# A fifth K pair with seven products in gate/up chunks 7 and 9, its sums of weights made during the output projection

## The chip, the cores and the metric

One core of a Trainium2 chip runs the whole program in one launch. The metric is the time on the device in microseconds. Beside the plain times there is one profiled execution; all views come from it.

## What is computed

A trunk of two layers over 256 tokens of width 2048, in float32. Each layer has a mixer (two kinds of attention) and a SwiGLU feed-forward part, each between two RMS norms:

```python
for l in range(DEPTH):                      # 2
    h = rms_norm(x, pre_mix_norm[l])
    m = hybrid_mixer(h, ...)                # h @ w_in, attention, @ w_o
    x = x + rms_norm(m, post_mix_norm[l])
    h = rms_norm(x, pre_ffn_norm[l])
    f = (silu(h @ w_gate[l]) * (h @ w_up[l])) @ w_down[l]
    x = x + rms_norm(f, post_ffn_norm[l])
```

The change is about `h @ w_gate` and `h @ w_up`: 256 x 2048 times 2048 x 5632, twice.

## The kernel before

**Products.** Weights come as tiles of 256 rows of K (a *pair* of 128-row blocks, `kp` 0 to 7 for K = 2048) by 512 columns, as [128, 2, 512] in SBUF. A float32 weight is split into a rounded part `hi` (ScalarE, a copy with rounding) and a rest `lo` (VectorE, weight minus `hi`); the activations are split likewise. One product of a 128-row block with 128 tokens is then three matmuls in `product` (lines 1051 to 1053): high by `hi`, high by `lo`, low by `hi`, each with 512 columns.

**Eight or seven products.** In the gate/up stage a *chunk* is 512 columns of gate and the same of up; there are 11 a layer. For each chunk and pair there are 2 blocks of K, 2 halves of the tokens and 2 weights: eight products, 24 matmuls (`eight`). For some pairs the kernel uses a scheme of the Strassen-Winograd kind with seven products, 21 matmuls (`seven`, `seven_products`). In place of gate and up it then multiplies the gate blocks and four sums of weights: T1 (gate's first block plus up's first), B22 (up's second block), T2 = B22 − T1, and T3, T4 = gate's blocks + T2; and on the token side four sums made once per pair (`pair_sums`, `token_sums`). `gate_sevens(c)` says which pairs: 4, 6 in chunk 0; 4, 5, 6 in chunk 1; 2, 4, 5, 6 in the others.

**How the sums of weights are made.** For a pair with seven products the gate tile goes to a buffer `G` (three of them) and the up tile to a buffer `T` (four), both by DMAs on SyncE's queue; a DMA of GpSimd with addition then adds gate's first block onto T's first (`summed`, lines 237 and 238). `mixed_weights` (lines 243 to 274) does the rest: `hi`, `lo` of G and of T; T2 in place in T (128x512, line 267); G plus T2 in place in G (128x1024, line 268); then `Th`, `Tl` of T2 (128x512) and of G (128x1024), lines 259 and 260. For a pair with eight products the two tiles go to `raw` buffers (four) and get `hi` and `lo` (lines 286 and 289), two 128x1024 operations each on ScalarE and VectorE. `hi` and `lo` have six buffers, `Th` and `Tl` two.

**Order.** All weights have one order of use, `weight_order`. `weights(i, ahead)` feeds the splits of tile i and of four tiles more. `fetch` issues their loads and looks four tiles further for sums (`EARLY`). Each engine works through its own instructions in a written order, which the framework's scheduler chose by priorities (program order) and its own estimates. Some edges are given by hand: `not_ahead` (a load for sums goes behind the load of the usual tile six places before it), `after_rests` (a VectorE operation goes behind the newest `lo`), `in_turn` (a load goes behind the newest load). A clock of *ticks*, advanced in the program every few matmuls, starts side jobs written as generators (`start`, `tick`).

**Around the stage.** The output projection comes first: 8 pairs of K for four chunks of 512 columns; two chunks in a first half (16 units of 12 matmuls, two ticks each), two in a second, in which two pairs have seven products. At its end the residual x is normed, transposed and split into the columns `xF` that the gate/up stage multiplies by (lines 455 and 460). A pool at the right end of SBUF holds 16 column tiles, first those of the input projection, then `xF`. Four "late rooms" of 4 KB a partition hold the halves of x until they are put away in DRAM in chunks 3 to 6, then the `act` tiles of the chunks from 7 on.

Of the kernel before, what the change touches and what calls it, by code (L numbers as in the profile page):

```python
# [9 lines left out]
F32 = mybir.dt.float32  # L10
# [7 lines left out]
P = 128  # L18
D = 2048
S = 256  # L20
# [23 lines left out]
FIRST_SEVEN = (4, 6)  # L44
FIRST_ORDER = (0, 1, 3, 2, 7, 4, 6, 5)
NEXT_SEVEN = (4, 5, 6)
FORM_AT = {(0, 1): 4, (0, 2): 6, (0, 5): 5, (1, 3): 2}
DOWN_SEVEN = ((4, 7, 10, 12, 15, 17, 20), (3, 5, 8, 10, 13, 15, 18))

WARM = 10  # L50
# [8 lines left out]
    return 0.8 - 0.6 * math.exp(-0.3 * layer)  # L59


def gate_sevens(c):

    return (FIRST_SEVEN, NEXT_SEVEN)[c] if c < 2 else SEVEN


# [87 lines left out]
def kernel(  # L154
# [42 lines left out]
    def fetch(upto):  # L197
        while len(raws) < min(upto, len(stream)):
            i = len(raws)
            for j in range(i, min(i + EARLY + 1, mix_raw[3])):  # L200
                if j in sevens and j not in sums:
                    summed(j)
            if i in sevens:
                raws.append(sums[i])
                continue
            if i + 1 in sevens:
                g = mix_raw[0].tile([P, 2, CW], F32, tag="G", bufs=mix_raw[1], name=f"G{i}")
                with not_ahead(i):
                    loads.append(nc.sync.dma_start(g, stream[i]))
# [12 lines left out]
            if not mixing:  # L222
                usual.append((i, loads[-1]))
# [5 lines left out]
        return tc.issue_after(next(load.ins for j, load in reversed(usual) if j <= i - LEAD))  # L229

    sums = {}

    def summed(i):

        sums[i] = mix_raw[0].tile([P, 2, CW], F32, tag="T", bufs=mix_raw[2], name=f"T{i}")
        with not_ahead(i):
            loads.append(nc.sync.dma_start(sums[i], stream[i]))
        nc.gpsimd.dma_start(sums[i][:, 0, :], stream[i - 1][:, 0, :], accum_op=ALU.add)  # L238
# [4 lines left out]
    def mixed_weights(i):  # L243

        g, u = raws[i - 1], raws[i]
        hi = wpool.tile([P, 2, CW], F32R, tag="hi", bufs=6, name=f"hi{i}")
        lo = wpool.tile([P, 2, CW], F32R, tag="lo", bufs=6, name=f"lo{i}")
        if i in own:
            th = wpool.tile([P, 2, CW], F32R, tag="hi", bufs=6, name=f"Th{i}")
            tl = wpool.tile([P, 2, CW], F32R, tag="lo", bufs=6, name=f"Tl{i}")  # L250
            th2 = mix_pool[0].tile([P, 2 * (S + P)], F32R, tag="ah", bufs=1, name=f"T2h{i}")[:, 0:CW]
            tl2 = mix_pool[0].tile([P, 2 * (S + P)], F32R, tag="al", bufs=1, name=f"T2l{i}")[:, 0:CW]
        else:
            th = mix_pool[0].tile([P, 3, CW], F32R, tag="Th", bufs=1 if i in plain else 2, name=f"Th{i}")
            tl = mix_pool[0].tile([P, 3, CW], F32R, tag="Tl", bufs=1 if i in plain else 2, name=f"Tl{i}")
            th2, tl2 = th[:, 2, :], tl[:, 2, :]

        def split(h, l, w):
            nc.scalar.activation(h, w, AF.Copy)  # L259
            nc.vector.tensor_tensor(out=l, in0=w, in1=h.bitcast(F32), op=ALU.subtract)  # L260

        if i in plain or i in own:
            with after_rests():
                nc.vector.tensor_tensor(out=u[:, 0, :], in0=g[:, 0, :], in1=u[:, 0, :], op=ALU.add)
        split(hi, lo, u)
        t2 = u[:, 1, :]
        nc.vector.tensor_tensor(out=t2, in0=t2, in1=u[:, 0, :], op=ALU.subtract)  # L267
        nc.vector.tensor_tensor(out=g, in0=g, in1=t2.unsqueeze(1).to_broadcast([P, 2, CW]), op=ALU.add)  # L268
        split(th2, tl2, t2)
        split(th[:, 0:2, :], tl[:, 0:2, :], g)  # L270
        t1, b22 = ((hi[:, k, :], lo[:, k, :]) for k in range(2))
        t3, t4 = ((th[:, k, :], tl[:, k, :]) for k in range(2))
        t2 = th2, tl2
        return {"b22": b22, "t1": t1, "t2": t2, "t3": t3, "t4": t4}

# [779 lines left out]
    def token_sums(pool, spool, bufs, a11, a12, a21, a22, nm, tags=("sh", "sl")):  # L1055

        s = pool.tile([P, 4, P], F32, tag="t2", name=f"s{nm}")
        nc.vector.tensor_tensor(out=s[:, 0, :], in0=a21, in1=a22, op=ALU.add)
        nc.vector.tensor_tensor(out=s[:, 1, :], in0=s[:, 0, :], in1=a11, op=ALU.subtract)
        nc.vector.tensor_tensor(out=s[:, 2, :], in0=a11, in1=a21, op=ALU.subtract)  # L1060
        nc.vector.tensor_tensor(out=s[:, 3, :], in0=a12, in1=s[:, 1, :], op=ALU.subtract)
        sh = spool.tile([P, 4, P], F32R, tag=tags[0], bufs=bufs, name=f"sh{nm}")
        nc.scalar.activation(sh, s, AF.Copy)
        sl = spool.tile([P, 4, P], F32R, tag=tags[1], bufs=bufs, name=f"sl{nm}")
        nc.vector.tensor_tensor(out=sl, in0=s, in1=sh.bitcast(F32), op=ALU.subtract)
        return [(sh[:, j, :], sl[:, j, :]) for j in range(4)]

# [30 lines left out]
    for l in range(L):  # L1098
# [15 lines left out]
        for n, (c, kp) in enumerate(plan[l]["order_o"][:16]):  # L1114
# [5 lines left out]
            if n in (9, 11):  # L1120
                kp = O_SEVEN[(n - 9) // 2]
                forms[kp] = pair_forms(pool, pool, 4, mix, kp, f"o{l}", tags=("tok", "tok"))
        xT = x_tiles(f"xF{l}")
        got = four_banks(True, [f"o{l}_{c}_{t}" for t in range(NT) for c in (2, 3)])
        accs = {(c, t): got[2 * t + c - 2] for c in (2, 3) for t in range(NT)}
        open_sums[0] = True
        for kp in LATE_O:
# [49 lines left out]
        def pair_sums(kp):  # L1177
            f = pool.tile([P, 2, S], F32, tag="t2", name=f"f{l}_{kp}")
            for kk in range(2):
                st = xT[2 * kp + kk]  # L1180
                nc.vector.tensor_tensor(out=f[:, kk, :], in0=st[:, 0, :].bitcast(F32), in1=st[:, 1, :].bitcast(F32), op=ALU.add)
            forms[kp] = token_sums(pool, gu, len(SEVEN), f[:, 0, 0:P], f[:, 1, 0:P], f[:, 0, P:S], f[:, 1, P:S], f"{l}_{kp}")
# [228 lines left out]
```

## Time and profile before

| | us |
|---|---|
| median of 3 runs | 2191.08 (2190.44 to 2192.06) |
| the profiled execution | 2190.85 |
| its span, first to last instruction | 2189.1 |
| input projection and attention, layer 0 | 0 to about 297 |
| output projection, layer 0 | about 297 to 391 |
| gate/up stage, layer 0 | about 402 to 860 |
| chunk 7 of it, by VectorE's last step of a chunk | 691.1 to 732.9 |
| chunk 9 of it | 774.6 to 816.4 |

In the views PE is TensorE's matmuls, PEld its loads of stationary tiles, DVE VectorE, ACT ScalarE, POOL GpSimd, SPq the DMA queue of SyncE. A row of a timeline has the start in us from the span's start, the duration, engine, line, operation, what it writes and reads, shapes and count; a bracket at its end gives how long the engine was idle before it and what ended the wait. A row of a group has busy time in us, the mean of one in ns, and the idle time before. Matmuls are pipelined, so that the duration of one is longer than the distance to the next.

### The profile page before, as it was taken

The numbers are of one execution on the slowest core, as the hardware profiler recorded it, in microseconds if no ns is written. First come the engines' busy times: TensorE is split into PE (matmuls) and PEld (weight loads), VectorE is DVE, ScalarE is ACT, GpSimd is POOL, SyncE is SP. The second block draws the span as 40 slices with busy tenths as digits, with TensorE's granted clock in tenths as the row PEclk, the third lists the DMA queues.
The fourth block names the chain that finished last, engine by engine and source line by source line (L and its number), as shares of the span: only waits on it lengthen the run. The fifth ranks groups of instructions, "written<-read, shape, count | busy, mean of one in ns | idle before, by whom it ended". The sixth has DMA issues, their size and how long they took to land.

```text
span 2189.1 us, 28547 instructions
## 1 busy us (share of the span) xinstructions
PE 2175.5 (99%) x9992; PEld 1789.9 (82%) x9992; DVE 1900.6 (87%) x2609; ACT 1371.9 (63%) x2053; POOL 139.2 (6%) x187
## 2 busy tenths in 40 slices
PE   9999999999999999999999999999999999999998
PEld 7888888888888888888878888888888888888886
DVE  7888658999999999989878886589999999999997
ACT  7666665766656656666665656657665666566664
POOL 2100000010010010000010000000000000100000
PEclk9999999999999999999999999999999999999999
DMA  9545554587687676767465555555867867767683
GB/s 331 184 164 173 192 187 170 186 276 230 223 270 228 200 257 203 248 207 261 147 241 173 182 175 182 193 170 193 274 209 252 254 214 232 234 213 234 207 265 100
DMA packets 138545, 467.28 MB, mean 213 GB/s; under 512 B 15760, under 2 KB 16784, under 8 KB 137888
## 3 DMA queue, kind: packets, MB, share of 16 engines
q1 hardware_dynamic: 121952, 436.03, 57.0%
q0 software_dynamic: 15872, 28.88, 7.5%
q8 instruction: 78, 1.28, 0.2%
q14 instruction: 67, 0.55, 0.1%
q10 hardware_dynamic: 576, 0.54, 0.1%
HBM read 457.00 MB, written 8.39 MB: 213 GB/s over the span
## 4 chain that ended last, share of the span: by engine, by line
PE 94%; DVE 3%; ACT 1%; DMA 1%; issue 1%; DVEq 0%; ACTq 0%
PE c L1052 9%; PE c L1053 9%; PE c L1051 9%; PE in L1051 7%; PE in L1053 7%; PE in L1052 7%; PE dn L1292 4%; PE dn L1295 4%; PE dn L1293 4%; PE p L1052 2%; PE p L1053 2%; PE p L1051 2%; PE o L536 2%; PE o L537 2%; PE o L538 2%; DVE lo L289 1%
## 5 line engine op out<-in xcount | busy, mean ns | idle before, releaser
L289 DVE TENSOR_TENSOR lo<-raw,hi 128x1024 fp32r<-128x1024 f32 x522 | 625.0, 1218 | 97.1 <-ACT hi L286 95.9
L286 ACT ACTIVATE hi<-raw 128x1024 fp32r<-128x1024 f32 x522 | 540.6, 1055 | 187.0 <-issue 51.4
L1051 PE MATMUL c<-hi,xF 128*128 128x512 f32 x834 | 328.0, 394 | 0.1
L1052 PE MATMUL c<-lo,xF 128*128 128x512 f32 x834 | 325.1, 390 | 0.7 <-DVE lo L289 0.7
L1053 PE MATMUL c<-hi,xF 128*128 128x512 f32 x834 | 324.8, 390 | 0.0
L238 POOL DMA_DIRECT2D T<-in_weights_in_turn_dram x110 | 95.8, 871 | 1681.6 <-PE c L1052 521.5
L1052 PEld LDWEIGHTS c<-lo,xF 128*128 128x128 f32 x834 | 156.7, 188 | 33.5 <-DVE lo L289 2.5
L1053 PEld LDWEIGHTS c<-hi,xF 128*128 128x128 f32 x834 | 156.6, 188 | 32.7
L1051 PEld LDWEIGHTS c<-hi,xF 128*128 128x128 f32 x834 | 156.7, 188 | 31.5 <-ACT xF L455 0.5
L1292 PE MATMUL dn<-hi,jh 128*128 128x512 f32 x432 | 168.2, 389 | 0.0
L1293 PE MATMUL dn<-lo,jh 128*128 128x512 f32 x432 | 168.1, 389 | 0.0
L289 DVE TENSOR_TENSOR lo<-G,hi 128x1024 fp32r<-128x1024 f32 x110 | 134.0, 1218 | 29.8 <-ACT hi L286 29.8
L259 ACT ACTIVATE hi<-T 128x1024 fp32r<-128x1024 f32 x110 | 115.5, 1050 | 41.1 <-PE c L1053 26.5
L259 ACT ACTIVATE Th<-G 128x1024 fp32r<-128x1024 f32 x110 | 116.1, 1055 | 39.0 <-DVE G L268 37.1
L260 DVE TENSOR_TENSOR Tl<-G,Th 128x1024 fp32r<-128x1024 f32 x110 | 133.9, 1217 | 5.3 <-ACT Th L259 5.3
L260 DVE TENSOR_TENSOR lo<-T,hi 128x1024 fp32r<-128x1024 f32 x110 | 133.9, 1217 | 2.6 <-ACT hi L259 2.2
L268 DVE TENSOR_TENSOR G<-G,T 128x1024 f32<-128x1024 f32 x110 | 134.3, 1221 | 2.1
L259 ACT ACTIVATE Th<-T 128x512 fp32r<-128x512 f32 x110 | 68.9, 626 | 105.0 <-DVE T L267 89.1
L1295 PE MATMUL dn<-hi,jl 128*128 128x512 f32 x432 | 132.9, 390 | 0.0
L1051 PE MATMUL in<-hi,xT 128*128 128x512 f32 x328 | 131.0, 401 | 1.5 <-ACT hi L856 1.5
L1051 PE MATMUL in<-hi,xI 128*128 128x512 f32 x328 | 131.1, 401 | 0.0
L1052 PE MATMUL in<-lo,xI 128*128 128x512 f32 x328 | 128.0, 390 | 0.3 <-DVE lo L289 0.3
(456 smaller groups left out, 4734.5 us busy)
## 6 DMA issues: line engine op xcount, KB each, us to landing
raw<-in_weights_in_turn_dram SPq DMA_DIRECT2D x522, 512.0 KB, 4.5
T<-in_weights_in_turn_dram SPq DMA_DIRECT2D x110, 512.0 KB, 6.3
G<-in_weights_in_turn_dram SPq DMA_DIRECT2D x110, 512.0 KB, 5.8
T<-in_weights_in_turn_dram POOLq DMA_DIRECT2D x110, 256.0 KB, 7.1
GU<-in_weights_in_turn_dram SPq DMA_DIRECT2D x32, 512.0 KB, 6.4
V<-in_weights_in_turn_dram SPq DMA_DIRECT2D x8, 512.0 KB, 4.2
away_ffn<-x SPq DMA_DIRECT2D x8, 512.0 KB, 8.5
xd<-away_ffn SPq DMA_DIRECT2D x8, 512.0 KB, 8.6
```

The source lines that it names most:

```text
L238: nc.gpsimd.dma_start(sums[i][:, 0, :], stream[i - 1][:, 0, :], accum_op=ALU.add)
L259: nc.scalar.activation(h, w, AF.Copy)
L260: nc.vector.tensor_tensor(out=l, in0=w, in1=h.bitcast(F32), op=ALU.subtract)
L268: nc.vector.tensor_tensor(out=g, in0=g, in1=t2.unsqueeze(1).to_broadcast([P, 2, CW]), op=ALU.add)
L286: nc.scalar.activation(hi, raw, AF.Copy)
L289: rest = nc.vector.tensor_tensor(out=lo, in0=raw, in1=hi.bitcast(F32), op=ALU.subtract)
L1051: nc.tensor.matmul(a, sh, hi, start=first, stop=False, skip_group_check=open_sums[0])
L1052: nc.tensor.matmul(a, sh, lo, start=False, stop=False, skip_group_check=open_sums[0])
L1053: nc.tensor.matmul(a, sl, hi, start=False, stop=last, skip_group_check=open_sums[0])
L1292: nc.tensor.matmul(accs[c, t], sh, hi[:, kk, :], start=first, stop=False, skip_group_check=open_sums[0])
L1293: nc.tensor.matmul(accs[c, t], sh, lo[:, kk, :], start=False, stop=False, skip_group_check=open_sums[0])
L1295: nc.tensor.matmul(accs[c, t], sl, hi[:, kk, :], start=False, stop=last, skip_group_check=open_sums[0])
```

## The change

Pair 3 also gets seven products, in chunks 7 and 9 of both layers. Its sums T1, T2, T3 and T4 for these two chunks are not made there. During the output projection a generator, `foresee`, started 8 ticks after the mixer's program, loads gate and up tiles of both, makes the sums in place on VectorE and stores them in a DRAM tile by GpSimd's DMAs. The four tiles for this lie in the pool of the columns, which is opened anew for them and once more for `xF`. In chunks 7 and 9 `summed` loads for such a pair T1 (from DRAM), B22 (from the weights) into one T buffer, T2 into a late room, and T3 with T4 into a second T buffer; GpSimd adds nothing, and VectorE only splits. These loads are issued at most one tile ahead instead of four. Gate's tile goes to G as for the other sevens. The token sums of pair 3 are made in chunk 6, and are kept in a late room.

```diff
+MORE_SEVEN = (2, 3, 4, 5, 6)
+MORE_AT = (7, 9)
+FORESEEN = {7: (3,), 9: (3,)}
+AHEAD_AT = 8
+AHEAD_PACE = 4
-FORM_AT = {(0, 1): 4, (0, 2): 6, (0, 5): 5, (1, 3): 2}
+FORM_AT = {(0, 1): 4, (0, 2): 6, (0, 5): 5, (1, 3): 2, (6, 3): 3}
...
 def gate_sevens(c):
 
+    if c in MORE_AT:
+        return MORE_SEVEN
...
-                if j in sevens and j not in sums:
+                if j in sevens and j not in sums and not (j in foreseen and j > i + 1):
                     summed(j)
...
+    def foresee(l):
+
+        jobs = [plan[l]["up"][c, kp] for c, kp in FORESEEN_PER_LAYER]
+        tiles = {}
+
+        def summed_up(i):
+            g, u = tiles[i]
+            k = kept.tile([P, 4, CW], F32, name=f"foreseen{i}")
+            with after_rests():
+                sums_in_place(g, u, True)
+            nc.gpsimd.dma_start(k[:, 0:2, :], u)
+            nc.gpsimd.dma_start(k[:, 2:4, :], g)
+            foreseen[i] = k
+
+        for n, i in enumerate(jobs):
+            tiles[i] = [x_pool[0].tile([P, 2, CW], F32, tag="W", bufs=2 * len(jobs), name=f"{q}{i}") for q in ("Gf", "Tf")]
+            for t, j in zip(tiles[i], (i - 1, i)):
+                with in_turn():
+                    nc.sync.dma_start(t, stream[j])
+                yield AHEAD_PACE
+            if n:
+                summed_up(jobs[n - 1])
+            yield AHEAD_PACE
+        yield AHEAD_PACE
+        summed_up(jobs[-1])
+
+    def sums_in_place(g, u, first):
+
+        t2 = u[:, 1, :]
+        if first:
+            nc.vector.tensor_tensor(out=u[:, 0, :], in0=g[:, 0, :], in1=u[:, 0, :], op=ALU.add)
+        nc.vector.tensor_tensor(out=t2, in0=t2, in1=u[:, 0, :], op=ALU.subtract)
+        nc.vector.tensor_tensor(out=g, in0=g, in1=t2.unsqueeze(1).to_broadcast([P, 2, CW]), op=ALU.add)
...
     def summed(i):
 
+        if i in foreseen:
+            kept_sums = foreseen[i]
+            n = len(found)
+            if n % len(FORESEEN_PER_LAYER) == 0:
+                thirds.append(late_room([P, 2, CW], f"second{i}"))
+            second = thirds[-1][:, n % 2, :]
+            two = [mix_raw[0].tile([P, 2, CW], F32, tag="T", bufs=mix_raw[2], name=f"{q}{i}") for q in ("T", "W")]
+            with not_ahead(i):
+                loads.append(nc.sync.dma_start(two[0][:, 0, :], kept_sums[:, 0, :]))
+                loads.append(nc.sync.dma_start(two[0][:, 1, :], stream[i][:, 1, :]))
+                loads.append(nc.sync.dma_start(second, kept_sums[:, 1, :]))
+                loads.append(nc.sync.dma_start(two[1], kept_sums[:, 2:4, :]))
+            sums[i] = two[0]
+            found[i] = second, two[1]
+            return
...
         split(hi, lo, u)
+        t1, b22 = ((hi[:, k, :], lo[:, k, :]) for k in range(2))
+        t3, t4 = ((th[:, k, :], tl[:, k, :]) for k in range(2))
+        if i in found:
+            second, w = found[i]
+            split(th2, tl2, second)
+            split(th[:, 0:2, :], tl[:, 0:2, :], w)
+            return {"b22": b22, "t1": t1, "t2": (th2, tl2), "t3": t3, "t4": t4}
...
-        sh = spool.tile([P, 4, P], F32R, tag=tags[0], bufs=bufs, name=f"sh{nm}")
+        if spool is None:
+            both = late_room([P, 2, 4, P], f"ss{nm}", F32R)
+            sh, sl = both[:, 0], both[:, 1]
+        else:
+            sh = spool.tile([P, 4, P], F32R, tag=tags[0], bufs=bufs, name=f"sh{nm}")
+            sl = spool.tile([P, 4, P], F32R, tag=tags[1], bufs=bufs, name=f"sl{nm}")
...
         mixer_in(pool, l, rs, xT, mix, mixed)
+        new_x_pool(f"ahead{l}")
+        start(foresee(l), AHEAD_AT)
...
-        xT = x_tiles(f"xF{l}")
...
+        new_x_pool(f"xF{l}")
+        xT = x_tiles(f"xF{l}")
         idx = plan[l]["o"][2, LAST_O[0]]
...
-            forms[kp] = token_sums(pool, gu, len(SEVEN), f[:, 0, 0:P], ...)
+            forms[kp] = token_sums(pool, gu if kp in SEVEN else None, len(SEVEN), f[:, 0, 0:P], ...)
```

More of the change, by code (lines that the diff above doesn't have):

```diff
@@ L59, in lambda_init @@
     return 0.8 - 0.6 * math.exp(-0.3 * layer)
+FORESEEN_PER_LAYER = [(c, kp) for c in FORESEEN for kp in FORESEEN[c]]
 def gate_sevens(c):
+    if c in MORE_AT:
+        return MORE_SEVEN
     return (FIRST_SEVEN, NEXT_SEVEN)[c] if c < 2 else SEVEN
@@ L231 @@
     sums = {}
-    def summed(i):
+    foreseen, found, thirds = {}, {}, []
+    def foresee(l):
[26 more added lines that the diff above has]
+        nc.vector.tensor_tensor(out=g, in0=g, in1=t2.unsqueeze(1).to_broadcast([P, 2, CW]), op=ALU.add)
+    def summed(i):
+        if i in foreseen:
[13 more added lines that the diff above has]
+            return
         sums[i] = mix_raw[0].tile([P, 2, CW], F32, tag="T", bufs=mix_raw[2], name=f"T{i}")
@@ L270, in mixed_weights @@
         split(th[:, 0:2, :], tl[:, 0:2, :], g)
-        t1, b22 = ((hi[:, k, :], lo[:, k, :]) for k in range(2))
-        t3, t4 = ((th[:, k, :], tl[:, k, :]) for k in range(2))
         t2 = th2, tl2
@@ L1143 @@
                     nc.vector.tensor_tensor(out=accs[c, 1], in0=accs[c, 1], in1=mg[1, 1][:, c - 2, :], op=shared_sign(1, c - 2))
+        assert all(plan[l]["up"][at] in foreseen for at in FORESEEN_PER_LAYER)
+        new_x_pool(f"xF{l}")
+        xT = x_tiles(f"xF{l}")
         idx = plan[l]["o"][2, LAST_O[0]]
@@ L1181, in pair_sums @@
                 nc.vector.tensor_tensor(out=f[:, kk, :], in0=st[:, 0, :].bitcast(F32), in1=st[:, 1, :].bitcast(F32), op=ALU.add)
-            forms[kp] = token_sums(pool, gu, len(SEVEN), f[:, 0, 0:P], f[:, 1, 0:P], f[:, 0, P:S], f[:, 1, P:S], f"{l}_{kp}")
+            forms[kp] = token_sums(pool, gu if kp in SEVEN else None, len(SEVEN), f[:, 0, 0:P], f[:, 1, 0:P], f[:, 0, P:S], f[:, 1, P:S], f"{l}_{kp}")
         def eight(banks, c, kp, toks, first, last):
```

1 line of the change is left out of this document (removed).

## The prediction

> **What bounds the kernel now.** I read the page first, then the windows cut by gate/up chunk, then the timelines of TensorE and VectorE inside one chunk. Part 1 of the page:
>
> ```profile
> span 2189.1 us, 28547 instructions
> PE 2175.5 (99%) x9992; PEld 1789.9 (82%) x9992; DVE 1900.6 (87%) x2609; ACT 1371.9 (63%) x2053; POOL 139.2 (6%) x187
> PE 94%; DVE 3%; ACT 1%; DMA 1%; issue 1%; DVEq 0%; ACTq 0%
> ```
>
> PE is busy all the time, and the chain that ended last (third line) is PE for 94%. So a matmul taken out is worth its pitch, if nothing else then comes late. VectorE is the candidate: 87% over the span, and more where the change works. Chunks 7 and 9 of layer 0 in the windows (columns: window, length, PE, PEld, DVE, ACT, POOL, clock, DMA share, GB/s):
>
> ```profile
> 691.10:732.90 41.80, 41.80 (x190) 34.61 (x190) 39.05 (x43) 25.29 (x29) 2.99 (x5) 1.00 0.70 224
> 774.60:816.40 41.80, 41.80 (x190) 34.62 (x190) 39.05 (x43) 25.29 (x29) 3.75 (x5) 1.00 0.70 226
> ```
>
> A chunk takes 41.8 us on a PE without gaps at full clock; DVE works 39.05 of them and has 2.7 us left. ACT is far from its limit.
>
> **What a pair is worth on PE.** First matmuls of pairs 3 (eight products, 24 matmuls), 4 (seven products, 21 matmuls) and 5 of chunk 7:
>
> ```profile
> 709.53 0.39 PE L1051 MATMUL c<-hi,xF 128*128 128x512 f32 x1
> 714.97 0.39 PE L1051 MATMUL p<-hi,xF 128*128 128x512 f32 x1
> 719.73 0.39 PE L1051 MATMUL p<-hi,xF 128*128 128x512 f32 x1
> ```
>
> Pair 3 takes 5.44 us, pair 4 takes 4.76: 0.2267 us a matmul either way (the 0.39 of a row overlaps its neighbours). The change turns pair 3 into a seven in chunks 7 and 9 of both layers: four pairs, 12 matmuls, **−2.72 us**, and that is all the change can take from PE. The Trainium skill, page "TensorE: Matmul & The Clock Gate", section "Back-to-back issue gap", gives some 131 ns as the sustained spacing of matmuls with 512 columns; by that the 12 would be worth an estimated 1.57 us. Those rows disagree at 227 ns, and the measurement decides.
>
> **What it costs on VectorE in the two chunks.** Timeline of DVE in chunk 7 around pairs 3 to 6, as it is:
>
> ```profile
> 700.20 2.35 DVE L289 TENSOR_TENSOR lo<-raw,hi 128x1024 fp32r<-128x1024 f32 x2
> ...
> 705.41 1.23 DVE L289 TENSOR_TENSOR lo<-G,hi 128x1024 fp32r<-128x1024 f32 x1 [1.73 <-ACT hi L286]
> ...
> 710.69 1.22 DVE L260 TENSOR_TENSOR lo<-T,hi 128x1024 fp32r<-128x1024 f32 x1
> 711.82 0.68 DVE L260 TENSOR_TENSOR Tl<-T,Th 128x512 fp32r<-128x512 f32 x1
> 712.43 1.22 DVE L260 TENSOR_TENSOR Tl<-G,Th 128x1024 fp32r<-128x1024 f32 x1
> ...
> 725.17 1.22 DVE L260 TENSOR_TENSOR Tl<-G,Th 128x1024 fp32r<-128x1024 f32 x1
> ```
>
> From start to start a 128x1024 operation takes 1.135 us (two in 2.27) and a 128x512 one 0.61. An eight costs DVE two of the former, 2.27 us (the first row is pair 3). The added pair comes with its sums made, so it has no add, subtract or broadcast add here: lo of the gate tile, lo of T1 and B22, Tl of T2 (128x512), Tl of T3 and T4 = 3 × 1.135 + 0.61 = 4.01 us, so +1.74 us. PE gives it 0.68 us less time: against PE, VectorE loses 2.42 us of lead at pair 3. A chunk's total still fits (39.05 + 1.74 = 40.8 us in 41.1), but where the lead runs out counts: three sevens in a row (4, 5, 6) eat it already. The last Tl of pair 6 (725.17 + 1.22 = 726.39) is read by
>
> ```profile
> 726.76 0.39 PE L1052 MATMUL p<-Tl,sh 128*128 128x512 f32 x1
> ```
>
> 0.37 us later. After the change five sevens stand in a row. What covers the loss is the 1.73 us in which DVE waits at 705.41 (there it is ahead as far as its buffers let it): 2.42 − 1.73 − 0.37 = **0.32 us late at pair 6, four times: +1.27 us**. Ends: nothing, if PE or VectorE take their work in another order (the lo's of pairs 7 and 0, which DVE does between pair 6's operations, aren't urgent); 2.42 − 0.37 = 2.05 a chunk, 8.2 us, if the idle isn't used. The nearest row where such a run did come late is chunk 1, pair 5:
>
> ```profile
> 471.63 0.40 PE L1053 MATMUL c<-hi,sl 128*128 128x512 f32 x1
> 472.50 0.50 PE L1052 MATMUL p<-Tl,sh 128*128 128x512 f32 x1 [0.48 <-DVE Tl L260]
> ```
>
> 873 ns where 227 are usual: 0.65 lost. My 0.32 is nearer to that than to the far end, so I take it.
>
> ACT gets one more 128x512 Th in such a chunk,
>
> ```profile
> L259 ACT ACTIVATE Th<-T 128x512 fp32r<-128x512 f32 x110 | 68.9, 626 | 105.0 <-DVE T L267 89.1
> ```
>
> 0.63 us, in 16 us that it has to spare: nothing.
>
> **Token sums of pair 3, made in chunk 6.** Nearest rows: the same sums of another pair early in the stage.
>
> ```profile
> 417.60 0.75 DVE L1181 TENSOR_TENSOR f<-xF 128x256 f32<-128x256 f32 x2
> 418.27 0.29 DVE L1060 TENSOR_TENSOR s<-f 128x128 f32<-128x128 f32 x1
> 418.47 0.29 DVE L1058 TENSOR_TENSOR s<-f 128x128 f32<-128x128 f32 x1
> ...
> 422.29 0.69 DVE L1065 TENSOR_TENSOR sl<-s,sh 128x512 fp32r<-128x512 f32 x1
> 422.89 1.22 DVE L268 TENSOR_TENSOR G<-G,T 128x1024 f32<-128x1024 f32 x1
> ```
>
> 0.67 + 4 × 0.20 + 0.60 = 2.07 us of DVE, once a layer. They go behind pair 3's rests, thus into the same 1.73 us of idle time: 0.34 over, against pair 6's 0.37 of lead. I take nothing. Ends: nothing, and 2.07 − 0.37 = 1.70 a layer if the idle is missed. Their place and that of T2 are late-room tiles; the saved halves of x that held these leave one by one in chunks 3 to 6, and the act tiles of chunks 7 and 8 find two free: no wait.
>
> **Sums made ahead, in the output projection.** Per layer: four 512 KB loads on SP, six DVE operations (2 × (0.61 + 0.61 + 1.135) = 4.7 us), four 512 KB stores on POOL. Beside them stand
>
> ```profile
> 297.00:391.00 94.00, 94.00 (x452) 78.75 (x451) 68.28 (x105) 55.04 (x109) 0.00 (x0) 1.00 0.51 171
> 354.02 2.35 DVE L289 TENSOR_TENSOR lo<-raw,hi 128x1024 fp32r<-128x1024 f32 x2
> 361.09 0.39 PE L537 MATMUL o<-lo,mix_sb 128*128 128x512 f32 x1
> ```
>
> 25 us of idle DVE, a POOL that does nothing, half of the DMA engines' time, and weights that are ready before they are used: the first lo of the row at 354.02 ends at 355.24, 5.85 us ahead of its matmul, in one of the tightest places of the stage. One set of sums is 2.36 us, less than that lead: nothing on PE. On SP the loads go behind the newest weight load, 0.4 us of issue each; on POOL nothing stands behind the stores until the first accumulate at 410.4 (row of L238, below). The end of it: 36 ticks after the start, 1.36 us each (six matmuls), some 50 us after 297, so about 350. The columns' tiles that take the place of the loaded ones are written from
>
> ```profile
> 392.65 0.37 ACT L455 ACTIVATE xF<-xT_ps,gains 128x128 fp32r<-128x128 f32 x1 [1.03 <-PE xT_ps L452]
> ```
>
> on, so that a store has some 40 us to land. Ends: nothing, and 2.36 us a layer, for the one set that would meet an exhausted lead.
>
> **Loads in chunks 7 and 9.** The added pair loads 512 KB for gate and 1.28 MB in four pieces on SP, 0.75 MB above an eight: 18 GB/s on 224. The buffers matter more: five sevens on three G buffers and four T buffers, of which pair 3 takes two. As it is, a released buffer is filled at once:
>
> ```profile
> 700.31 0.33 SPq L237 DMA_DIRECT2D T<-in_weights_in_turn_dram  x1
> 703.71 0.33 SPq L209 DMA_DIRECT2D G<-in_weights_in_turn_dram  x1
> 704.47 0.89 POOL L238 DMA_DIRECT2D T<-in_weights_in_turn_dram  x1 [10.20 <-DMA T<-in_weights_in_turn_dram]
> T<-in_weights_in_turn_dram SPq DMA_DIRECT2D x110, 512.0 KB, 6.3
> G<-in_weights_in_turn_dram SPq DMA_DIRECT2D x110, 512.0 KB, 5.8
> T<-in_weights_in_turn_dram POOLq DMA_DIRECT2D x110, 256.0 KB, 7.1
> ...
> L238 POOL DMA_DIRECT2D T<-in_weights_in_turn_dram x110: 857/866/889, 410.4 to 2126.8; - x110
> ```
>
> Those at 700.31 and 703.71 are the buffers that pair 2 gives back; today they serve later pairs (the T even the next chunk). Afterwards pair 5 gets them, and on SP the raw loads of pairs 7 and 0 stand behind that T's wait, whose lo's DVE needs only from 719 on. Its G lands at 703.71 + 5.8 = 709.5. Its T: the load landed about 704 here (POOL's wait ended at 704.47), then 7.1 us: 711.6; by the medians throughout 700.31 + 6.3 + 0.65 + 7.1 = 714.4. DVE reads that T at 710.69 today, for a matmul after 721. I take it as covered: DVE has Tl, Tl of pair 4 to do first (711.82 and 712.43, 1.75 us). The price where it isn't is rival 2.
>
> **Sum.** 2190.85 (profiled execution: span 2189.1 and 1.75 around it) − 2.72 + 1.27 + 0 = 2189.4. The median of the runs, 2191.08, lies 0.23 above the profiled one: **2189.6**.
>
> **Rivals.**
>
> 1. *All of the saving arrives.* Pair 6 isn't late since the order shifts: 2190.85 − 2.72 + 0.23 = 2188.4. For it: lo's of later pairs stand between pair 6's operations and could wait; against: 0.37 us of lead.
> 2. *Pair 5's T is late, slower than before.* ACT and DVE take their work in a written order. If lo of T5 stays ahead of pair 4's Tl's and T5 lands at 714.4, ACT's hi (1.05) and lo end at 716.6 instead of 711.9: 4.7 us late, with all behind it. Pair 6 then misses PE by up to 4.7 − 0.37 = 4.3 us a chunk, 17 us in all, 2205.6; half of that, 2197, if the order gives way. It decides from a T5 landing after 712. For it: two buffers less, POOL's accumulate behind the load, the accumulate's 7.1 us, which come on top of the load's 6.3; against: 700.31 to 711.6 in the one case seen, and 1.75 us of other work. The Trainium skill, page "SBUF — State Buffer", section "Who interferes with whom", has a rule that would make POOL worse here: a VectorE operation in a two-port mode locks GpSimd out for its whole length, so that its DMAs are issued late. The trace doesn't bear it out: POOL's 110 issues take 857 to 889 ns each beside a DVE that is 93% busy in such a chunk (39.05 of 41.8); the chance stays.
> 3. *The idle isn't used but the loads hold*, one late Tl as in chunk 1 in every one of four chunks and then another at pair 5, about 1.2 us each: 2190.85 − 2.72 + 4.7 + 0.23 = 2193.1. Not to be told from no change.
> 4. *PE's idle time where the stage begins shrinks*, as the order of work there changes. It has waits such as
>
> ```profile
> 401.56 0.50 PE L1052 MATMUL c<-lo,xF 128*128 128x512 f32 x1 [0.35 <-DVE lo L289]
> ```
>
> It takes 1.9 us beyond all of the saving to be faster by over 0.2%. Nothing in the change aims there.
>
> That the change doesn't do what it says I can leave out: the products are counted in the program.
>
> **Chances.** Forecast 0.44, rival 1 0.24, rival 3 0.12, rival 2 0.17, rival 4 0.03. A measurement of this kernel can tell about 0.2% (4.4 us) from no change: below 2186.7 is faster, above 2195.5 slower. Only rival 4 is faster (0.03), rival 2 is slower (0.17), the rest, 0.80, within. Range: from a little under rival 1, 2187.8, to 2.05 us in each of four chunks, 2190.85 − 2.72 + 8.2 + 0.23 = 2196.6; it leaves out most of rival 2 and rival 4.
>
> **What would show it.** PE with 9980 instructions. In chunks 7 and 9 pair 3 at 4.76 us, and between pairs 5 and 7 gaps over 0.227 of a few tenths with a DVE Tl as releaser; the 1.73 us of DVE idle ahead of pair 4's first lo gone there and smaller in chunk 6; chunks of 41.1 to 41.5 us. POOL's four stores before 370, and no wait of the first columns (392) on them. The prediction is wrong if ACT's hi of pair 5's T waits on a DMA for over 2 us, if PE waits in chunk 6 or in the output projection, or if chunk 8 or 10 doesn't return to 41.8.

## The result, and the profile after

The changed kernel takes 2201.5 us (median of five runs, 2198.66 to 2202.23); the kernel before, on the same chip, 2191.06 (five runs, 2190.34 to 2192.06). The ratio is **1.0046, 95% interval 1.0035 to 1.0058**: slower. That is 11.9 us above the forecast, outside its range (2187.8 to 2196.6), and between the two ends of rival 2 (2197 and 2205.6). The profiled execution took 2202.23 us, 11.38 more than that of before.

The first lines of the page after:

```profile
span 2200.5 us, 28641 instructions
PE 2179.4 (99%) x9980; PEld 1788.0 (81%) x9980; DVE 1919.0 (87%) x2643; ACT 1377.0 (63%) x2063; POOL 143.7 (7%) x195
```

The 12 matmuls are gone, yet the span is longer. The starts of chunks 7, 8, 9 and 10 of layer 0, from TensorE's timeline, tell where:

```profile
694.10 0.39 PE L1116 MATMUL c<-hi,xF 128*128 128x512 f32 x1
739.15 0.39 PE L1116 MATMUL c<-hi,xF 128*128 128x512 f32 x1
780.88 0.39 PE L1116 MATMUL c<-hi,xF 128*128 128x512 f32 x1
823.45 0.39 PE L1116 MATMUL c<-hi,xF 128*128 128x512 f32 x1
```

The same way, for all chunks that changed (a chunk of five sevens on a PE that never waits would take 41.73 − 3 × 0.2267 = 41.05 us):

| us from first matmul to first matmul of the next chunk | layer 0 before | after | layer 1 before | after |
|---|---|---|---|---|
| chunk 1 | 43.67 | 44.03 | 43.71 | 44.15 |
| chunk 6 (token sums of pair 3) | 41.77 | 42.15 | 41.77 | 42.19 |
| chunk 7 (fifth seven) | 41.73 | 45.05 | 41.73 | 45.45 |
| chunk 8 | 41.77 | 41.73 | 41.73 | 41.77 |
| chunk 9 (fifth seven) | 41.73 | 42.57 | 41.73 | 43.49 |

Chunk 7 gives +7.04 over both layers, chunk 9 +2.60, chunks 1 and 6 +0.80 each: 11.2 of the 11.4 us. Each of the four changed chunks is longer than before, though it has three matmuls less.

Chunks 7 and 9 of layer 0 in the windows (columns as in the prediction: window, length, PE, PEld, DVE, ACT, POOL, clock, DMA share, GB/s):

```profile
694.10:739.15 45.05, 42.27 (x186) 33.78 (x185) 40.73 (x45) 26.67 (x32) 4.36 (x5) 1.00 0.73 239
780.88:823.45 42.57, 41.67 (x186) 33.85 (x185) 40.05 (x44) 25.95 (x31) 4.29 (x5) 1.00 0.67 223
```

VectorE works 40.73 us of 45.05 in chunk 7, which would fit into 41.05. So the amount of work alone doesn't make the chunk long (experiment 3 tests this); what remains is when the work is done. What PE waits for there, from its timeline (start, length, the idle time before it and its releaser):

```profile
717.28 0.39 PE L1118 MATMUL q<-hi,sl 128*128 128x512 f32 x1
718.89 0.49 PE L1116 MATMUL p<-Th,sh 128*128 128x512 f32 x1 [1.23 <-ACT Th L319]
720.15 0.50 PE L1117 MATMUL p<-Tl,sh 128*128 128x512 f32 x1 [0.77 <-DVE Tl L320]
...
730.39 0.73 PE L1116 MATMUL p<-Th,sh 128*128 128x512 f32 x2 [0.65 <-ACT Th L319]
```

From 717.28 to 718.89 and on to 720.15 pass 1.61 and 1.26 us where 0.227 are usual: 2.4 us lost at pair 4. The rest of the chunk's 4.0 (45.05 − 41.05) goes around 730, at pair 6.

Who was late? ScalarE's and VectorE's timelines ahead of that moment:

```profile
707.55 1.07 ACT L351 ACTIVATE hi<-G 128x1024 fp32r<-128x1024 f32 x1
714.30 1.06 ACT L319 ACTIVATE hi<-T 128x1024 fp32r<-128x1024 f32 x1 [5.68 <-DMA T<-in_weights_in_turn_dram]
...
717.78 1.06 ACT L319 ACTIVATE Th<-G 128x1024 fp32r<-128x1024 f32 x1 [0.96 <-DVE G L335]
```

```profile
710.86 0.68 DVE L334 TENSOR_TENSOR T<-T 128x512 f32<-128x512 f32 x1
715.39 1.22 DVE L320 TENSOR_TENSOR lo<-T,hi 128x1024 fp32r<-128x1024 f32 x1 [3.85 <-ACT hi L319]
716.53 1.22 DVE L335 TENSOR_TENSOR G<-G,T 128x1024 f32<-128x1024 f32 x1
717.67 0.68 DVE L320 TENSOR_TENSOR Tl<-T,Th 128x512 fp32r<-128x512 f32 x1
...
718.87 1.23 DVE L320 TENSOR_TENSOR Tl<-G,Th 128x1024 fp32r<-128x1024 f32 x1
```

Read it backwards from the matmul at 718.89. It needs Th of pair 4's G (ends 718.84). That needs the broadcast add into G (716.53 to 717.75), whose inputs were ready at 711.54, when the subtract of the row at 710.86 ended. But in VectorE's order the add stands behind lo of **pair 5's** T (715.39), which needs ScalarE's hi of that T (714.30), which waited 5.68 us for a DMA. Pair 4's work, needed at once and ready, stood behind pair 5's, not needed yet and not there. The Trainium skill, page "TensorE: Matmul & The Clock Gate", section "Architectural detail: the array is 16× 32×32, not 1× 128×128", says that ScalarE and VectorE work their queues strictly first in, first out; the add that was ready at 711.54 and began at 716.53 agrees.

This order isn't that of the kernel before. There the same add stands ahead of lo of pair 5's T (710.69 in the prediction's rows):

```profile
709.54 1.23 DVE L268 TENSOR_TENSOR G<-G,T 128x1024 f32<-128x1024 f32 x1
```

So in chunk 7 two things came together: a later T of pair 5, and a written order in which pair 4's add waits behind it. Why the scheduler chose that order no run shows.

Why pair 5's T came late, on SP's queue and on POOL:

```profile
703.28 1.46 SPq L297 DMA_DIRECT2D T<-in_weights_in_turn_dram  x2
```

```profile
708.27 0.88 POOL L298 DMA_DIRECT2D T<-in_weights_in_turn_dram  x1 [14.96 <-DMA T<-in_weights_in_turn_dram]
```

Its load starts at 703.28, when VectorE has read pair 2's T for the last time (Tl of T, 702.57 to 703.25); POOL's add on top is issued at 708.27 and lands about 714.1, 20.0 us into the chunk. The other three changed chunks show the same wait, in ScalarE's hi of pair 5's T (one row each: chunk 9 of layer 0, 7 and 9 of layer 1):

```profile
799.78 1.06 ACT L319 ACTIVATE hi<-T 128x1024 fp32r<-128x1024 f32 x1 [4.38 <-DMA T<-in_weights_in_turn_dram]
1808.71 1.06 ACT L319 ACTIVATE hi<-T 128x1024 fp32r<-128x1024 f32 x1 [5.95 <-DMA T<-in_weights_in_turn_dram]
1895.32 1.06 ACT L319 ACTIVATE hi<-T 128x1024 fp32r<-128x1024 f32 x1 [5.34 <-DMA T<-in_weights_in_turn_dram]
```

But in chunk 9 pair 4's add stands ahead of lo of pair 5's T, as in the kernel before (layer 0 below; in layer 1 they start at 1892.08 and 1896.41):

```profile
797.49 1.23 DVE L335 TENSOR_TENSOR G<-G,T 128x1024 f32<-128x1024 f32 x1
800.87 1.23 DVE L320 TENSOR_TENSOR lo<-T,hi 128x1024 fp32r<-128x1024 f32 x1 [2.16 <-ACT hi L319]
```

In chunk 9 PE waits nowhere for a Th. Pair 4 loses nothing in layer 0; in layer 1 one distance between its matmuls is 0.57 us instead of 0.227. What chunk 9 loses goes at pairs 5 and 6, where PE waits for VectorE's Tl.

### The profile page after: what moved, and what is told of

It is laid out like the page before. It is cut to its first block, busy times and chain, and to the rows that moved or that the text cites. A ratio compares the mean times of both kernels' runs of the same rounds, so it can differ in the third digit from the quotient of the medians.

```text
span 2200.5 us, 28641 instructions
## 1 busy us (share of the span) xinstructions
PE 2179.4 (99%) x9980; PEld 1788.0 (81%) x9980; DVE 1919.0 (87%) x2643; ACT 1377.0 (63%) x2063; POOL 143.7 (7%) x195
## 4 chain that ended last, share of the span: by engine, by line
PE 85%; DVE 7%; DMA 4%; issue 2%; ACT 2%; SPq 0%; DVEq 0%; ACTq 0%; POOLq 0%
PE c L1117 8%; PE c L1118 8%; PE c L1116 8%; PE in L1116 7%; PE in L1118 7%; PE in L1117 7%; PE dn L1365 4%; PE dn L1368 4%; PE dn L1366 4%; DMA T<-in_weights_in_turn_dram 2%; PE o L601 2%; PE o L602 2%; PE o L603 2%; PE p L1117 2%; PE p L1118 2%; DVE lo L354 2%
## 5 line engine op out<-in xcount | busy, mean ns | idle before, releaser
L354 DVE TENSOR_TENSOR lo<-raw,hi 128x1024 fp32r<-128x1024 f32 x514 | 615.5, 1219 | 93.5 <-ACT hi L351 92.4
L351 ACT ACTIVATE hi<-raw 128x1024 fp32r<-128x1024 f32 x514 | 531.9, 1055 | 177.7 <-DMA raw<-in_weights_in_turn_dram 47.9
L1116 PE MATMUL c<-hi,xF 128*128 128x512 f32 x806 | 317.2, 394 | 0.1
L1117 PE MATMUL c<-lo,xF 128*128 128x512 f32 x806 | 314.3, 390 | 0.7 <-DVE lo L354 0.7
L1118 PE MATMUL c<-hi,xF 128*128 128x512 f32 x806 | 313.9, 390 | 0.0
L1117 PEld LDWEIGHTS c<-lo,xF 128*128 128x128 f32 x806 | 151.5, 188 | 32.5 <-DVE lo L354 2.6
L1118 PEld LDWEIGHTS c<-hi,xF 128*128 128x128 f32 x806 | 151.3, 188 | 31.6
L1116 PEld LDWEIGHTS c<-hi,xF 128*128 128x128 f32 x806 | 151.4, 188 | 30.5 <-ACT xF L520 0.5
L354 DVE TENSOR_TENSOR lo<-G,hi 128x1024 fp32r<-128x1024 f32 x114 | 138.9, 1218 | 20.6 <-ACT hi L351 20.5
L320 DVE TENSOR_TENSOR lo<-T,hi 128x1024 fp32r<-128x1024 f32 x114 | 138.8, 1218 | 16.1 <-ACT hi L319 15.6
L319 ACT ACTIVATE Th<-G 128x1024 fp32r<-128x1024 f32 x110 | 116.1, 1056 | 43.5 <-DVE G L335 42.3
L351 ACT ACTIVATE hi<-G 128x1024 fp32r<-128x1024 f32 x114 | 120.1, 1053 | 36.6 <-PE c L1118 19.8
L1117 PE MATMUL in<-lo,xT 128*128 128x512 f32 x328 | 127.9, 391 | 0.6 <-DVE lo L923 0.6
```

The lines of the kernel that those rows point to most:

```text
L351: nc.scalar.activation(hi, raw, AF.Copy)
L354: rest = nc.vector.tensor_tensor(out=lo, in0=raw, in1=hi.bitcast(F32), op=ALU.subtract)
L1116: nc.tensor.matmul(a, sh, hi, start=first, stop=False, skip_group_check=open_sums[0])
L1117: nc.tensor.matmul(a, sh, lo, start=False, stop=False, skip_group_check=open_sums[0])
L1118: nc.tensor.matmul(a, sl, hi, start=False, stop=last, skip_group_check=open_sums[0])
```

## The experiments

The theory (A): the added pair takes two of the four T buffers, so pair 5's T is loaded too late, and ScalarE and VectorE stop at it with ready work of pair 4 behind. Its rivals: (V) five sevens in a row are more than VectorE can do in time, whatever the buffers; (O) the sums ahead in the output projection and their stores cost time; (G) it is the three G buffers, not the T's. Each time stands beside the kernel before on the same chip in the same batch, with the 95% interval of the ratio.

**1. Sums made ahead, not used.** Output projection, stores and chunk 6's token sums as in the changed kernel; chunks 7 and 9 with four sevens as before.

```
-        if c in MORE_AT:
-            return MORE_SEVEN
```

> The sums are made ahead and stored, and pair 3's token sums are made in chunk 6, but chunks 7 and 9 use eight products for pair 3 as before the change, so what was stored isn't used (the computation is that of the kernel before). Theory A (pair 3 holds two of the four T buffers in chunks 7 and 9, so pair 5's T arrives late and ScalarE waits for it with pair 4's work behind): the 11 us are gone, 2191 to 2192.5, with 0.4 us in each of chunks 6 and 1 at most. Rival O (the loads, sums, stores and token sums ahead cost the time): 2197 or more. Rival V (VectorE can't do five sevens in a row): as A, 2191 to 2192.5.

Measured: 2192.57 us beside 2190.98, ratio 1.0007 (0.9998 to 1.0016), an interval that holds no change. Chunks 7 to 9 take 41.73, 41.77 and 41.73 us, chunk 6 42.19 in layer 0 and 42.44 in layer 1. So the sums ahead cost no more than can be measured (O falls as the cause); chunk 6 keeps its 0.4 to 0.7, which is the token sums.

**2. Five sevens with an ordinary fifth.** Nothing made ahead; pair 3 of chunks 7 and 9 makes its sums in place, with *more* VectorE work than in the changed kernel: a subtract and a broadcast add, 0.61 + 1.135 us.

```
-FORESEEN = {7: (3,), 9: (3,)}
+FORESEEN = {}
...
-        start(foresee(l), AHEAD_AT)
```

> Nothing is made ahead; pair 3 in chunks 7 and 9 is a seven like the others, with one T buffer and its sums made in place. VectorE has 1.73 us more work a chunk than in the changed kernel. Theory A: five T on four buffers, so pair 6's T and not pair 5's waits for pair 2's; little or no wait of ScalarE's hi on a T, but VectorE is over its limit (39.05 + 3.47 = 42.5 us of work for 41.1 of PE): 42.3 to 43.3 us a chunk, 2193 to 2198. Rival V: worse than the changed kernel in proportion to the work, chunks of 45 us and more, over 2202.

Measured: 2191.93 us beside 2190.98, ratio 1.0006 (0.9997 to 1.0015). Chunks 7, 8 and 9 of layer 0 in its windows:

```profile
694.18:735.71 41.53, 41.53 (x186) 33.79 (x185) 40.88 (x45) 27.02 (x32) 2.63 (x3) 1.00 0.66 194
735.71:777.71 42.00, 42.00 (x189) 34.42 (x188) 40.58 (x46) 25.67 (x31) 5.23 (x6) 1.00 0.88 269
777.71:819.02 41.31, 41.31 (x187) 33.86 (x185) 40.88 (x45) 26.51 (x31) 2.63 (x3) 1.00 0.64 199
```

VectorE is busy 40.88 us of 41.53 and the chunk loses 0.5, not 4. V falls: the same run of sevens, with more work, goes through when each takes one T buffer. The time expected under A (2193 to 2198, 42.3 to 43.3 us a chunk) was too high as well: VectorE does only 40.88 of the expected 42.5 us of work within the chunk, and chunk 8 takes 42.00 us where before has 41.77. VectorE's written order around pair 5 is also another here, so this run doesn't separate buffers from order.

**3. The added pair's T tiles elsewhere.** The changed kernel, but the two tiles of pair 3 come from the four raw buffers instead of the T buffers.

```
-            two = [mix_raw[0].tile([P, 2, CW], F32, tag="T", bufs=mix_raw[2], ...) for q in ("T", "W")]
+            two = [wpool.tile([P, 2, CW], F32, tag="raw", bufs=4, ...) for q in ("T", "W")]
```

> The changed kernel, with pair 3's two tiles of sums in the raw buffers that pair 3 as an eight would have used, so that the four T buffers serve pairs 2, 4, 5, 6 as before. Gate's tile of pair 3 stays in G. Theory A: no wait on a T, chunks 7 and 9 at 41.1 to 41.8 us, 2189 to 2192. Rival V: VectorE's work is the same, so chunks stay at 43 to 45 us, 2199 to 2202. Rival G (three G buffers for five sevens): ScalarE waits on G instead, 2194 to 2200.

Measured: **2189.06 us** (2187.71 to 2189.95) beside 2190.98, ratio 0.9992 (0.9983 to 1.0001). Its windows of chunks 7 and 9:

```profile
692.95:734.20 41.25, 41.25 (x187) 33.93 (x185) 40.74 (x45) 27.00 (x32) 4.29 (x5) 1.00 0.77 259
775.97:817.01 41.04, 41.04 (x186) 34.01 (x185) 40.61 (x45) 26.93 (x32) 3.12 (x4) 1.00 0.73 233
```

and ScalarE's hi of pair 5's T:

```profile
709.09 1.06 ACT L319 ACTIVATE hi<-T 128x1024 fp32r<-128x1024 f32 x1 [1.66 <-PE c L1118]
```

It starts 16.1 us into the chunk instead of 20.2 and waits for a buffer that PE gives back, no more for a DMA. VectorE does what it did (40.74 us against 40.73), PE without a gap. The written order around it is that of the changed kernel, lo of pair 5's T ahead of pair 4's add:

```profile
710.31 1.22 DVE L320 TENSOR_TENSOR lo<-T,hi 128x1024 fp32r<-128x1024 f32 x1
711.44 1.22 DVE L335 TENSOR_TENSOR G<-G,T 128x1024 f32<-128x1024 f32 x1
```

With the T there in time, this order costs at most 0.2 us (41.25 instead of 41.05). The 12.4 us between this median and the changed kernel's come from where two tiles lie.

**4. Only the G tile elsewhere**, and **5. both elsewhere.** The rival G: the changed kernel with pair 3's G in the raw buffers and its T's left; and the kernel of 3 with the G moved as well. In 5 the loads of pair 3's sums are also issued one tile later, right behind its gate tile (`j > i` in place of `j > i + 1` in `fetch`).

```
-            if i + 1 in sevens:
+            if i + 1 in sevens and i + 1 not in foreseen:
```

> The changed kernel with gate's tile of pair 3 in a raw buffer, its two tiles of sums still in T buffers. Theory A (T): no better than the changed kernel, 2198 to 2203, ScalarE's hi still waits 4 to 6 us on pair 5's T. Rival G (five sevens on three G buffers): 2189 to 2193.

Measured: 2201.82 us (2200.28 to 2202.99) beside 2190.68, ratio 1.0046 (1.0032 to 1.0059), the changed kernel's own ratio. ScalarE's row is the old one:

```profile
712.43 1.06 ACT L319 ACTIVATE hi<-T 128x1024 fp32r<-128x1024 f32 x1 [5.43 <-DMA T<-in_weights_in_turn_dram]
```

> As the one before, and gate's tile of pair 3 in a raw buffer too, so that G, T are used by pairs 2, 4, 5, 6 alone as before the change; a pair 3 takes three raw buffers instead of two, and its sums are loaded right behind its gate tile. Theory A: chunks 7 and 9 at 41.1 to 41.5 us, 2188.4 to 2190.5, faster than before by up to 0.12%. Rival V: 2199 to 2202. Rival G: well below the run before this.

Measured: 2189.07 us beside 2190.98, ratio 0.9993 (0.9984 to 1.0002), as in 3; chunk 7 41.23, chunk 9 41.05. G falls: moving the G changes neither the changed kernel nor the kernel of 3 by more than the intervals.

**6. The order alone.** Buffers and loads as in the changed kernel, pair 5's T as late; but in chunks 7 and 9 ScalarE's hi and VectorE's lo of it are put behind pair 4's last Th and Tl.

```
-        split(hi, lo, u)
+        split(hi, lo, u, newest_split[0] if i in behind_last else None)
```

with the activation in `split` under `tc.issue_after(after[0].ins)`, the subtract under `tc.issue_after(after[1].ins)`, and `behind_last` holding pair 5 of chunks 7 and 9.

> The changed kernel with two edges more in chunks 7 and 9: ScalarE's hi of pair 5's T behind the last Th of pair 4, and VectorE's lo of it behind the last Tl of pair 4. The buffers and loads stay, T5 lands as late as in the changed kernel (20 us into chunk 7). If the price is that pair 4's sums stand behind a tile that hasn't landed: chunk 7 falls from 45.1 to 41.5 to 42.5 us, total 2190 to 2195. If the late tile alone is the price, whatever stands behind it: chunks as in the changed kernel, 2199 to 2202.

Measured: **2190.78 us** (2189.1 to 2192.28) beside 2190.68, ratio 0.9996 (0.9987 to 1.0005). POOL's add on pair 5's T comes as late as ever, 13.8 us into the chunk (14.2 in the changed kernel):

```profile
707.31 0.88 POOL L298 DMA_DIRECT2D T<-in_weights_in_turn_dram  x1 [15.16 <-DVE Tl L325]
```

VectorE and ScalarE now spend the wait on pair 4:

```profile
710.24 0.68 DVE L339 TENSOR_TENSOR T<-T 128x512 f32<-128x512 f32 x1
710.96 1.22 DVE L340 TENSOR_TENSOR G<-G,T 128x1024 f32<-128x1024 f32 x1
712.10 0.68 DVE L325 TENSOR_TENSOR Tl<-T,Th 128x512 fp32r<-128x512 f32 x1
713.31 1.23 DVE L325 TENSOR_TENSOR Tl<-G,Th 128x1024 fp32r<-128x1024 f32 x1 [0.53 <-ACT Th L323]
714.45 1.22 DVE L325 TENSOR_TENSOR lo<-T,hi 128x1024 fp32r<-128x1024 f32 x1
```

```profile
712.21 1.06 ACT L323 ACTIVATE Th<-G 128x1024 fp32r<-128x1024 f32 x1 [0.54 <-DVE G L340]
713.20 1.06 ACT L323 ACTIVATE hi<-T 128x1024 fp32r<-128x1024 f32 x1
```

The broadcast add starts 17.5 us into the chunk instead of 22.4, and Th of pair 4 with it; lo of pair 5's T is done 22.2 us in instead of 22.5, no later than before the reordering. Chunk 7 falls from 45.05 to 41.21 (layer 1: 45.45 to 41.85), chunk 9 to 41.09 in both. So the late tile by itself costs 0.2 us in chunk 7 of layer 0 and 0.8 in layer 1. Experiment 3 takes away the lateness and leaves the order, this one takes away the order and leaves the lateness, and each brings chunk 7 back: the price was, above all, the late tile **with ready work behind it in the queue**, not either of them alone.

**7. The kernel before with two T buffers in gate/up instead of four** (one run). The supposed cause, in every chunk, without the change.

```
-        ... ("G", 3, [P, 2, CW]), ("T", 4, [P, 2, CW])):
+        ... ("G", 3, [P, 2, CW]), ("T", 2, [P, 2, CW])):
...
-        mix_raw[:] = gu, 3, 4, plan[l]["down"][0, 0]
+        mix_raw[:] = gu, 3, 2, plan[l]["down"][0, 0]
```

> The kernel before the change with two T buffers in the gate/up stage instead of four, all else the same. Theory A: this is what pairs 2, 4, 5, 6 have left in chunk 7 of the changed kernel, now in every chunk: a T is loaded only when one two sevens earlier is read, 13 to 14 us before it can be used; chunks of 2 to 10 on both layers at 44 to 50 us, 2230 to 2350. Rival (a late T costs little by itself, the change of order from other causes is what counts): chunks near 42 us, below 2210.

Measured: 2325.76 us, chunks 2 to 10 between 46.08 and 50.35 us where before has 41.7 to 41.9. ScalarE's hi of a T again waits for the DMA:

```profile
700.86 1.06 ACT L259 ACTIVATE hi<-T 128x1024 fp32r<-128x1024 f32 x1 [4.50 <-DMA T<-in_weights_in_turn_dram]
```

It speaks for A, but roughly: here the shortage lasts, so the loads themselves are too few at a time, and not only their order counts.

**8. Token sums later.** The kernel of 3, with pair 3's token sums at step 7 of chunk 6 instead of step 3.

```
-FORM_AT = {..., (6, 3): 3}
+FORM_AT = {..., (6, 7): 3}
```

> The run with pair 3's sums in raw buffers, and with pair 3's token sums called for ahead of pair 7 of chunk 6 instead of pair 3 of chunk 6, so that they fall into the next chunk's eights. If they come late against pair 6 in chunk 6 (0.42 us there): chunk 6 back to 41.77, 2188.2 to 2188.8. If their cost only moves: chunk 6 or 7 longer by 0.3 to 0.4 us, 2189 as before.

Measured: 2189.6 us beside 2190.68, ratio 0.9992 (0.9983 to 1.0001). Chunk 6 is back at 41.73, but chunk 7 takes 41.70 and 41.51 and chunk 8 42.09 and 41.87. The 0.4 us are moved, not removed.

**9 and 10. A fifth seven in three chunks.** The experiments point to a version with more of the same: kernels 3 and 5 with chunk 8 added (three sets made ahead a layer).

```
-MORE_AT = (7, 9)
-FORESEEN = {7: (3,), 9: (3,)}
+MORE_AT = (7, 8, 9)
+FORESEEN = {7: (3,), 8: (3,), 9: (3,)}
...
-AHEAD_PACE = 4
+AHEAD_PACE = 3
...
-            n = len(found)
-            if n % len(FORESEEN_PER_LAYER) == 0:
+            n = len(found) % len(FORESEEN_PER_LAYER)
+            if n % 2 == 0:
```

> The run with pair 3's sums in raw buffers, with chunk 8 as a third chunk with five sevens (three pairs made ahead a layer, the side job's steps three ticks apart instead of four, a second late room for T2). If a chunk with five sevens gives its 0.68 us also between two others: chunks 7, 8, 9 at 41.05 to 41.3 us, 2187.2 to 2188.5. If VectorE needs a chunk with four sevens in between to recover its lead (40.8 us of work for 41.1): chunk 9 at 41.8 or more, 2189 or more.

> As the one before, with gate's tile of pair 3 in a raw buffer too. As before 2187.2 to 2188.5; if three raw buffers for a pair 3 delay the next eights' loads, chunk 8 and 9 longer by some tenths, 2188.5 to 2190.

Measured: 2188.02 us (2187.19 to 2189.77), ratio 0.9988 (0.9979 to 0.9997), and 2188.16 us (2186.87 to 2188.77), ratio 0.9984 (0.9975 to 0.9993), beside 2191.45. Chunks 7, 8 and 9 of layer 0 take 41.21, 41.31 and 41.05 us in the first and 41.21, 41.09 and 41.05 in the second, so VectorE needs no chunk with four sevens in between. The page of the first counts 9974 matmuls, 18 less than before: 18 × 0.2267 = 4.1 us were to be had; the medians of the two show 3.4 and 3.3, and both intervals lie below 1. They are the fastest of the kernels here, by less than what a measurement of this kernel tells with ease.

## Why the prediction was wrong, point by point

- **−2.72 from the matmuls: right.** 9992 to 9980. With the wait gone, chunk 9 of experiment 3 takes 41.04 us against 41.05 worked out.
- **+1.27, VectorE 0.32 late in each changed chunk: right in kind, somewhat high.** In experiment 3 the chunks of five sevens lose 0.20 and 0 (layer 0), 0.22 and 0.04 (layer 1): 0.46 in all. With the ordinary fifth (experiment 2) they lose 0.48 and 0.26 in layer 0, and chunk 8 between them 0.23. The 1.73 us of idle time ahead of pair 4's first lo were indeed used; VectorE's timeline of the changed kernel has no gap there:

```profile
706.32 1.22 DVE L320 TENSOR_TENSOR Tl<-W,Th 128x1024 fp32r<-128x1024 f32 x1
707.45 1.22 DVE L354 TENSOR_TENSOR lo<-G,hi 128x1024 fp32r<-128x1024 f32 x1
```

- **Token sums in chunk 6 at nothing: too low.** +0.38 and +0.42, within the ends of 0 and 1.70. Chunk 1's +0.36 and +0.44, which I had not forecast, is not explained by any run; the chunk shifts with every kernel here, between about 42.9 us (layer 0 of experiment 3) and 44.7 (layer 1 of experiment 6), so it needn't belong to this change.
- **Sums ahead at nothing: right.** The stores of layer 0 went off before 370, the last at 363 where about 350 was worked out. The first column is written 0.35 us later than before (393.00 against 392.65), after the same wait for PE and not for a store. The last two stores:

```profile
360.68 0.53 POOL L254 DMA_DIRECT2D foreseen<-Tf  x1 [13.02 <-DVE Tf L275]
362.95 0.53 POOL L255 DMA_DIRECT2D foreseen<-Gf  x1 [1.74 <-DVE Gf L276]
```

- **"I take it as covered: DVE has Tl, Tl of pair 4 to do first": this step failed.** The wait was put at nothing; the four changed chunks take 12.4 us more than four times 41.05, of which 0.5 remain in experiment 3 (and some 1.7 came with a fall of the clock, last section). The cover doesn't exist. The row quoted in the prediction said so: lo of T (710.69) stood *ahead of* both Tl's (711.82 and 712.43), in the written order. Work that stands behind the waiting instruction covers nothing; it pays. In chunk 7 the broadcast add of pair 4 paid too, since the new order put it behind. Experiment 6 makes the sentence true by two order edges, and then the step costs 41.21 − 41.05 = 0.2 us in chunk 7 of layer 0 (0.8 in layer 1). The sign that the prediction named for being wrong, ScalarE's hi of pair 5's T waiting on a DMA for over 2 us, stands in all four chunks (4.38 to 5.95 us).
- **The landing of pair 5's T: between the two estimates, by errors that offset each other.** Counted from the chunk's first matmul (692.97 before, 694.10 after) the single case, 711.6, is 18.6 us, the medians, 714.4, are 21.4, and measured are 20.0. The load began 1.84 us later in the chunk than assumed (9.18 instead of 7.34), because VectorE came later to pair 2's Tl; load and add then took 10.9 us, less than the 11.3 of the single case and the 14.1 of the medians.
- **Rival 2 was what happened**: named mechanism, named threshold ("a T5 landing after 712", 19.0 us into the chunk). Its price per chunk, up to 4.3 us, is close to the 4.0 and 4.4 of chunk 7 (1.5 and 2.4 in chunk 9), but partly by luck: it placed the loss at pair 6, and 2.4 of the 4.0 us were lost at pair 4, behind the add, which it didn't count among the work held up. It had 0.17 where its own condition was met by the estimate from medians.
- **The rule on POOL** that stood beside it (the Trainium skill, page "SBUF — State Buffer", section "Who interferes with whom") played no part, and the prediction applied it wrongly: the same section says that `tensor_tensor`, the operation in VectorE's rows around these issues, has no two-port mode. The trace agrees: POOL's four stores of layer 0 were issued in 0.53 to 0.59 us and the add on pair 5's T in 0.88, as before.
- **ScalarE, one Th more at nothing: a miscount without consequence.** The added pair needs two more than an eight, of 128x512 and of 128x1024 (rows at 701.54 and 702.06 in chunk 7, 0.62 and 1.05 us). ScalarE's work grew from 25.29 to 26.67 us a chunk, still far from the chunk's length. Of the same kind: the 1.9 us in rival 4 are 1.7 (2188.4 − 2186.7).
- **Chunks 8 and 10 back at 41.8**: right, the delay isn't passed on.

What stays open: how much of chunk 9's smaller loss comes from its order (the add ahead of lo of pair 5's T) and how much from the earlier T (asked for 7.3 us into the chunk instead of 9.2, landed after 18.7 us instead of 20.0 in layer 0). In layer 1 it lands only some 0.6 us earlier than in chunk 7, and PE's waits at pair 4 fall from 1.49 and 0.76 us to one of 0.18, which speaks for the order; the two weren't tried apart. Whether another pair of order edges would also remove the 0.8 of layer 1's chunk 7 in experiment 6 wasn't tried either.

## What to carry to other kernels

When a change takes buffers from a pool that others share, date the refill (release + load + what is added on top, by the medians) and then read, on each engine that reads it, what stands *behind* that read in the written order: those are the ones that pay, and what stands ahead covers nothing once it is done. A wait of 5.7 us on ScalarE, an engine 63% busy, cost TensorE 4 us in chunk 7 because ready work stood behind it. The remedy may be a buffer from a pool with slack (experiment 3) or only another place in the queue (experiment 6); here either one was enough. Read the order anew after a change: in chunk 7 the scheduler had also moved an operation behind the wait.

## What was unexpected of the hardware

Chunk 7 takes 45.45 us in layer 1 and 45.05 in layer 0. Windows of the changed kernel around the stall, two in layer 0 and then three in layer 1 (the third number from the end is TensorE's granted clock):

```profile
715.47:718.89 3.42, 2.20 (x10) 1.50 (x8) 3.42 (x5) 2.46 (x4) 0.00 (x0) 1.00 0.40 68
718.89:722.30 3.41, 2.64 (x10) 1.99 (x11) 3.41 (x5) 3.40 (x4) 0.00 (x0) 1.00 0.34 106
```

```profile
1811.15:1814.56 3.41, 1.17 (x4) 0.39 (x3) 3.41 (x5) 2.45 (x4) 0.00 (x0) 1.00 0.00 0
1814.60:1817.50 2.90, 2.90 (x7) 2.32 (x8) 2.90 (x4) 2.12 (x3) 0.00 (x0) 0.50 0.52 181
1817.50:1821.00 3.50, 3.50 (x15) 2.88 (x15) 3.50 (x4) 1.69 (x2) 0.00 (x0) 0.93 0.00 0
```

In layer 1 the granted clock falls to 0.50 after the stall, from 1814.6 to 1818.0, and the matmuls come at half the pace (7 in 2.90 us); then the pace is the old one (15 in 3.50). In layer 0 a stall of the same kind leaves the clock at 1.00. The two waits of PE in layer 1 were

```profile
1813.30 0.50 PE L1116 MATMUL p<-Th,sh 128*128 128x512 f32 x1 [1.49 <-ACT Th L319]
1814.56 0.79 PE L1117 MATMUL p<-Tl,sh 128*128 128x512 f32 x1 [0.76 <-DVE Tl L320]
```

The Trainium skill, page "TensorE: Matmul & The Clock Gate", section "HAM oscillation — how this bites in real kernels", gives as a rule that no idle gap should be over some 3.4 us. Here the clock fell after gaps of 1.49 and 0.76 us with one matmul between, and didn't after gaps of 1.23 and 0.77 us in layer 0. The drop lasts 3.41 us, and the times between two changes of the granted clock are whole multiples of 3.413 us in the traces here (378.88 and 1809.06 us in this one). In the stretch of that length just ahead of the drop PE is busy for 1.17 us; with the same division carried back to layer 0, the stall there falls into two stretches, with 2.20 and 2.64 us busy. Experiment 4 has the same drop in chunk 7 of layer 1, after a stretch with 1.75 us busy. That the busy time in a stretch decides, and not the longest gap, fits these figures, but no run was made to vary it. The slow matmuls cost some 1.7 us (eight distances of 0.37 to 0.59 us instead of 0.227); chunk 7 of layer 1 is only 0.4 us longer than that of layer 0 because PE then has no wait at pair 6, where layer 0 lost 1.3 us.
